# The branch projections and the output multiply of a hybrid encoder step on float16 parts instead of float32r parts, with powers of two found on the chip

## The chip, the cores and the metric

The kernel runs on one core of one Trainium2 chip. The metric is the device time of one execution in microseconds, as the median of several. A core has a matrix engine (TensorE, PE in the profile; its weight loads are the row PEld), a vector engine (VectorE, DVE), a scalar engine (ScalarE, ACT), a third elementwise engine (GpSimd, POOL) and SyncE (SP), which issues the transfers between the chip's memory and the core's on-chip buffer SBUF. PE writes its results to PSUM, a small buffer that is divided here into named banks ("a", "b", "c", "pj" and others). Each engine works its own list of instructions in order; between engines, semaphores say what may start.

## The reference

One layer of a streaming encoder, for a prompt of 2048 rows and 32 decode rows, 1024 columns wide, in float32. A projection `w_in` makes the inputs of two branches and two gates; branch A is attention over a band of chunks, branch B a gated delta rule. What concerns this change is the end:

```python
qa, ka, va, za, qkv_b, zb, a_b, b_b, gate_a, gate_b = split_projection(x @ w_in)
...
ya = (oa.reshape(bsz, t, A_WIDTH) * jax.nn.silu(za)) @ w_branch_a
...
yb = (ob * jax.nn.silu(zb)) @ w_branch_b

mix = jax.nn.sigmoid(gate_a) * ya + jax.nn.sigmoid(gate_b) * yb
y = layer_norm(ALPHA * x + mix @ w_out, ln_g, ln_b)
```

`oa * silu(za)` and `ob * silu(zb)` are called the gated values here, 512 wide each, and `mix` the merged values. `w_branch_a` and `w_branch_b` (512 x 1024) are `w_a` and `w_b` in the kernel, `w_out` is 1024 x 1024.

## The kernel before

**How the work is recorded.** Every part of the kernel is a Python generator. A small planner (class `Flow`, L155) keeps an estimated clock for each of them and for each engine, and runs the one whose clock is lowest; each instruction that it calls is recorded through one helper (L260, so that almost every row of the profile has this line) and priced by `Engine.price`. The order on each engine is therefore the order that these estimates give, fixed when the program is built. `mark` is an event, `gate(n)` a count of free buffers, `bank[...]` the gates of PSUM.

**Stages.** The rows are worked in two halves of 1024. In each half, first the jobs of branch B (phase B), then those of attention (phase A): a job is 128 columns of `w_in`, fetched (`fetch`, L585) into one of two raw slots of 512 KB, split by `divide` (L623) and multiplied by `multiply` (L664). The projections are already on float16 parts: a value is scaled by a power of two, rounded to float16 (hi), and the rest rounded again (lo); the product is hi x hi + hi x lo + lo x hi. `power` (L359) finds the power of two: ACT squares and sums each partition, a PE matmul with a constant (`tiny`) sums over the partitions, DVE adds a small number, POOL raises to the power of -1/2, and DVE masks all but the exponent.

**The merge.** When half 1's phase A is near its end, `fetch` brings `w_a` and `w_b` through the raw slots (four rows of 128 x 1024 each); `split_w` (L726) and `split` (L717) make their parts `whi` and `wlo`: ACT rounds to float32r (written `fp32r` or `f32` in rows), and POOL (even row k) or DVE (odd k) subtracts. `claim_w` (L731) waits until the buffers of both parts of h are free before it lays w_b's parts there. `last_weights` (L1962) does the same with `w_out`, in 16 pieces of 128 x 512, into `woh` and `wol`, and then loads the four layer-norm rows `l0g`, `l0b`, `lng`, `lnb`. `merge` (L2049) then works 8 blocks of 256 rows, the last of 288 with the decode rows:

- `load_g` (L2027) fetches the block's gated values of both branches, `split_g` (L2018) splits them into `ghi` and `glo`, one buffer each.
- 16 groups (f = 0 to 7, two branches) of 12 matmuls in bank "a", which has three buffers: four times whi.ghi and wlo.ghi, then four times whi.glo. DVE evacuates each with (sig + 1) x PSUM into the tile `sg` that holds the gate's values.
- `fold` (L2058): when both branches of f are there, DVE adds them (`sg<-sg`), ACT rounds the sum (`mh`), and DVE (even f) or POOL (odd f) subtracts (`ml`); `ms` holds the same for the 32 decode rows.
- the output multiply: for each 128 rows and each half of the columns (banks "pj" and "b") 24 matmuls of 512 columns, woh.mh and wol.mh for k = 0 to 7, then woh.ml. In the last block the decode rows come first, with 16 matmuls per half.
- `finish` (L2183): DVE adds PSUM times 0.5 to the row tile `xt` and does the layer norm (`lng`, `lnb`), and the row is stored.

`x_load` (L2168) prepares `xt` ahead: DVE scales the input row by its own mean and deviation (`xt<-xt,mv`), then POOL multiplies by `l0g` and adds `l0b`, two operations on 128 x 1024 one behind the other.

## Time and profile before

| | |
|---|---|
| median of 3 runs (2081.7 to 2089.64) | 2084.61 us |
| the profiled execution | 2083.65 us |
| its span, first to last instruction | 2081.6 us |
| mean granted TensorE clock | 0.988 |
| PE, DVE, ACT, POOL busy, share of the span | 95%, 72%, 47%, 30% |
| start of merge block 1 / 3 / 7 on PE | 1742.82 / 1835.30 / 2016.29 us |

Times in the profile are microseconds from the start of the span. A row of the timeline gives the start, the time, the engine, the line and the instruction with its output and inputs; in square brackets stand the idle time of the engine ahead of it and what ended that. A group's row gives the count, the busy time, the mean of one in ns, and the idle time ahead of the group's instructions. PE's matmuls are pipelined, so that their times overlap.

### The profile page before, as it was taken

What the parts mean: (1) busy time and instruction counts of PE and PEld (TensorE: products, weight loads), DVE (VectorE), ACT (ScalarE), POOL (GpSimd) and SP (SyncE); (2) the same over time, 40 slices, a digit from 0 to 9 for tenths busy, and PEclk for the clock granted to TensorE, in tenths of its full rate; (3) what the DMA queues carried; (4) which work ended last, traced back from release to release, by engine and by line L of the source; (5) the groups of instructions that cost most, each with busy time, mean ns of one, the idle gap of its engine ahead of it and who ended that gap; (6) DMA issues with size and microseconds to landing.
All of it is one profiled execution on the core that took longest, in us unless ns stands there. A gap on an engine that the chain in (4) does not pass through costs nothing. (4 is left out here: it accounts for less than half of the span.)

```text
span 2081.6 us, 41386 instructions
## 1 busy us (share of the span) xinstructions
PE 1968.6 (95%) x15098; PEld 1411.3 (68%) x15098; DVE 1499.7 (72%) x4661; ACT 978.1 (47%) x2098; POOL 633.1 (30%) x708
## 2 busy tenths in 40 slices
PE   4999999999999999998999999999999988999998
PEld 3454666766465657566667777667666777888996
DVE  7679889873377758679998986356656667666775
ACT  5565554444466667564544543355656641111110
POOL 6244333422312113243332331311011134433342
PEclk9999999999999999999999999999999999999999
DMA  3233232323423233122233233332232445433331
GB/s 119 72 92 106 75 102 57 100 80 91 116 86 111 70 92 100 65 85 72 66 89 83 77 99 84 105 92 76 72 88 88 129 137 175 132 102 122 102 116 54
DMA packets 197719, 196.49 MB, mean 94 GB/s; under 512 B 79622, under 2 KB 147570, under 8 KB 197516
## 3 DMA queue, kind: packets, MB, share of 16 engines
q1 hardware_dynamic: 197516, 193.85, 31.6%
q8 instruction: 119, 1.95, 0.4%
q14 instruction: 84, 0.69, 0.1%
HBM read 135.91 MB, written 50.53 MB: 90 GB/s over the span
## 5 line engine op out<-in xcount | busy, mean ns | idle before, releaser
L260 PE MATMUL pj<-hi,whi 128*128 128x512 f16 (+2 forms) x1992 | 644.8, 339 | 10.4 <-DVE zb L260 2.7
L260 PE MATMUL pj<-hi,wlo 128*128 128x512 f16 (+2 forms) x1952 | 635.9, 338 | 2.4 <-POOL wlo L260 2.3
L260 PEld LDWEIGHTS <-whi 128*128 128x128 f16 x3984 | 413.5, 105 | 214.5 <-issue 3.9
L260 PE MATMUL pj<-lo,whi 128*128 128x512 f16 (+2 forms) x1992 | 457.7, 340 | 0.0
L260 POOL TENSOR_TENSOR wlo<-wraw,whi 128x512 f16<-128x512 f32 x192 | 226.9, 1184 | 585.9 <-ACT whi L260 313.0
L260 PEld LDWEIGHTS <-wlo 128*128 128x128 f16 x1952 | 204.8, 105 | 111.1 <-issue 10.7
L260 ACT CAST mh<-sg 128x256 fp32r<-128x256 f32 x64 | 25.9, 406 | 279.6 <-DVE sg L260 279.6
L260 ACT CAST ph<-b 128x512 f16<-128x512 f32 (+2 forms) x224 | 93.1, 421 | 100.0 <-PE b L260 96.8
L260 DVE TENSOR_TENSOR pl<-b,ph 128x512 f16<-128x512 f32 (+2 forms) x224 | 107.7, 485 | 44.7 <-ACT ph L260 43.1
L260 PE MATMUL a<-ghi,whi 128*128 128x256 f32 (+1 forms) x512 | 132.6, 290 | 6.3 <-DVE sg L260 6.2
L260 DVE TENSOR_TENSOR sys_u<-sys_u,sys_t 128x60 f32<-128x60 f32 (+23 forms) x527 | 129.3, 251 | 6.7
L260 ACT ACTIVATE wraw<-wraw,w_scale 128x1024 f32<-128x1024 f32 (+1 forms) x98 | 111.5, 1138 | 46.6 <-DVE w_scale L260 42.9
L260 PE MATMUL a<-ghi,wlo 128*128 128x256 f32 (+1 forms) x512 | 130.3, 285 | 0.0
L260 ACT CAST whi<-wraw 128x512 f16<-128x512 f32 (+1 forms) x196 | 119.4, 612 | 20.9 <-PE pj L260 18.0
L260 DVE TENSOR_TENSOR sys_t<-sys_u,sys_p 128x60 f32<-128x60 f32 (+21 forms) x459 | 121.2, 265 | 6.1
L260 ACT ACTIVATE sb<-sb,mx,unit 128x640 f32<-128x640 f32 (+4 forms) x128 | 108.8, 851 | 20.0 <-DVE mx L260 19.7
L260 DVE SCALAR_TENSOR_TENSOR acc<-raw,cwT,acc 128x512 f32<-128x512 f32 x144 | 114.0, 792 | 5.4 <-ACT acc L260 4.4
L260 POOL TENSOR_TENSOR w_scale<-w_scale,mhalf 128x1 f32<-128x1 f32 x49 | 30.9, 631 | 269.3 <-DVE w_scale L260 204.2
L260 PE MATMUL b<-ident,sb 128*128 128x128 f32 x560 | 100.6, 279 | 5.3 <-ACT sb L260 2.2
L260 PEld LDWEIGHTS a<-ghi,whi 128*128 128x128 f32 x512 | 98.0, 191 | 9.0 <-DVE sg L260 7.8
L260 ACT COPY v_t<-o 128x64 f32<-128x64 f32 x132 | 27.7, 210 | 161.1 <-PE o L260 133.3
L260 PEld LDWEIGHTS a<-ghi,wlo 128*128 128x128 f32 x512 | 97.8, 191 | 0.3
(350 smaller groups left out, 4221.8 us busy)
## 6 DMA issues: line engine op xcount, KB each, us to landing
wraw<-in_w_in SPq DMA_DIRECT2D x192, 256.0 KB
sg<-sig SPq DMA_DIRECT2D x112, 128.0 KB
sig<-sig SPq DMA_DIRECT2D x44, 256.0 KB
sys_p<-sol_p SPq DMA_DIRECT2D x17, 512.0 KB
x<-in_x_p SPq DMA_DIRECT2D x16, 512.0 KB
xt<-in_x_p SPq DMA_DIRECT2D x16, 512.0 KB
out_y_p<-xt SPq DMA_DIRECT2D x16, 512.0 KB
glo<-g SPq DMA_DIRECT2D x14, 512.0 KB
```

Source lines behind the costliest of these rows:

```text
L260: r = f(*a, **k)
```

## The change

All float32r parts become float16 parts, which need a power of two ahead of the rounding:

- **w_a and w_b**: each row k has its own power, `b_scale` (a Square with a sum into `b_sq`, `power`), its reciprocal `b_inv`, and the least of the four, `b_min` (`weigh`). w_a's four rows and eight extra fetches of w_out (`measure_o`, which only squares and sums them for the one power `o_scale`) are fetched between the jobs of half 1's phase A, one ahead of each of twelve jobs, through the same raw slots. w_b is fetched behind the jobs as before, but waits for only one of the two buffers of h.
- **w_out**: split with `o_scale`, all 16 `wo` tiles in one pool.
- **gated values**: `load_g` has two buffers for the parts and a raw tile per branch. ACT squares both branches (into the parts' low buffers, which are overwritten later), `power` takes both sums at once, and the least of power x `b_min` gives the block's unit; each row k of the gated values is scaled by unit x `b_inv`, so that all products of a group have one scale.
- **merged values**: scaled by the constant `MSMALL` (2^-18). `finish` multiplies by a value per block that undoes all this, instead of 0.5.
- **the split** itself: for odd k, ACT writes the scaled hi and DVE makes lo in one operation (x times scale minus hi); for even k, ACT scales in place, ACT rounds, and POOL subtracts. The low parts `ml` and `ms` are now all made by DVE.

```diff
-    def power(out, sums):
+    def power(out, sums, n=1):
...
+        more = [measure_o] * KD + [split_a] * NP
         for job in jobs:
+            if job.half and job.key and job.key[0] == 0 and job.key[1] > 0:
+                f = more.pop(0)
+                if f is split_a and len(more) == NP - 1:
+                    yield from claim_w(0)
...
+                yield raw_gate
+                raw = wpool.tile([P, KD, P], F32, tag="wraw", bufs=NRAW, name="raw_more")
+                raw = raw[:].rearrange("p k n -> p (k n)")
+                flow.start(f(k, raw, dma(raw, (w_a if f is split_a else w_out)[k * P:(k + 1) * P, :])))
+                yield
...
-        for br, w in enumerate((w_a, w_b)):
-            yield from claim_w(br)
...
+        yield from claim_w(1)
+        for k in range(NP):
...
+            flow.start(split_w(1, k, wr, dma(wr, w_b[k * P:(k + 1) * P, :])))
...
+    def measure_o(k, raw, t):
+        yield t
+        S.activation(out=raw, in_=raw, func=AF.Square, accum_out=o_sq[:, k:k + 1])
+        raw_gate.give()
+        o_left[0] -= 1
+        if not o_left[0]:
+            yield
+            V.tensor_reduce(out=o_sq[:, KD:], in_=o_sq[:, 0:KD], axis=AX.X, op=ALU.add)
+            yield
+            yield from power(o_scale[:, 0:1], o_sq[:, KD:])
...
+    def split(hi, lo, x, sc, eng, m):
+
+        if eng is V:
+            S.activation(out=hi, in_=x, func=AF.Copy, scale=sc)
+            m[0].done()
+            yield
+            V.scalar_tensor_tensor(out=lo, in0=x, scalar=sc, in1=hi, op0=ALU.mult, op1=ALU.subtract)
+        else:
+            S.activation(out=x, in_=x, func=AF.Copy, scale=sc)
+            yield
+            S.copy(out=hi, in_=x)
+            m[0].done()
+            yield
+            G.tensor_tensor(out=lo, in0=x, in1=hi, op=ALU.subtract)
+        m[1].done()
...
+        S.activation(out=lo[:, k], in_=wr, func=AF.Square, accum_out=sq)
+        yield
+        yield from power(sc, sq)
+        flow.start(weigh(br, k))
+        for c in range(2):
+            cs = slice(c * 512, (c + 1) * 512)
+            yield from split(hi[:, k, cs], lo[:, k, cs], wr[:, cs], sc, V if k % 2 else G,
+                             (mark(), w_ready[br, k, c]))
+            yield
+        raw_gate.give()
...
     def claim_w(br):
         if br:
-            for g in h_free:
-                yield g
+            yield h_free[0]
...
-    g_slot, m_slot, x_slots = gate(1), gate(1), gate(3)
+    g_slot, m_slot, x_slots = gate(2), gate(1), gate(3)
...
+                S.activation(out=glo[:, :, 0:n], in_=raw[:, :, 0:n], func=AF.Square, accum_out=gs[:, br:br + 1])
+                yield
+
+            yield from power(gs[:, 2:4], gs[:, 0:2], 2)
+            for k in b_known:
+                yield k
+            V.tensor_tensor(out=gs[:, 2:4], in0=gs[:, 2:4], in1=b_min[:], op=ALU.mult)
+            yield
+            V.tensor_reduce(out=gs[:, 4:5], in_=gs[:, 2:4], axis=AX.X, op=ALU.min)
...
-                eng = G if f % 2 else V
-                S.copy(out=mh[:, f], in_=parts[0][:, 0:FB])
+                S.activation(out=mh[:, f], in_=parts[0][:, 0:FB], func=AF.Copy, scale=MSMALL)
                 m_ready[0][f].done()
                 yield
-                eng.tensor_tensor(out=ml[:, f], in0=parts[0][:, 0:FB], in1=mh[:, f].bitcast(F32), op=ALU.subtract)
+                V.scalar_tensor_tensor(out=ml[:, f], in0=parts[0][:, 0:FB], scalar=MSMALL, in1=mh[:, f], op0=ALU.mult,
+                                       op1=ALU.subtract)
...
-            V.scalar_tensor_tensor(out=xt[:rows, cs], in0=part, scalar=0.5, in1=xt[:rows, cs],
+            V.scalar_tensor_tensor(out=xt[:rows, cs], in0=part, scalar=unit[:rows], in1=xt[:rows, cs],
```

The planner sets the order of everything anew from the first extra fetch on (about 1325 us). Three places matter below.

DVE in a merge block in the middle, around the scaling of the first of its two row tiles, before (`sg<-sg,a` evacuates a group, `sg<-sg` adds the branches):

```order
L260 TENSOR_SCALAR xt<-xt,mv 128x1024
L260 SCALAR_TENSOR_TENSOR sg<-sg,a 128x256
L260 TENSOR_TENSOR sg<-sg 128x256
L260 SCALAR_TENSOR_TENSOR sg<-sg,a 128x256
L260 TENSOR_TENSOR sg<-sg 128x256
L260 TENSOR_TENSOR ml<-sg,mh 128x256
L260 SCALAR_TENSOR_TENSOR sg<-sg,a 128x256 x2
```

and the same place after the change:

```order
L262 TENSOR_SCALAR xt<-xt,mv 128x1024
L262 SCALAR_TENSOR_TENSOR sg<-sg,a 128x256
L262 SCALAR_TENSOR_TENSOR ml<-sg,mh 128x256
L262 TENSOR_TENSOR sg<-sg 128x256
L262 SCALAR_TENSOR_TENSOR ml<-sg,mh 128x256
L262 SCALAR_TENSOR_TENSOR sg<-sg,a 128x256 x3
L262 TENSOR_TENSOR sg<-sg 128x256
```

Between two evacuations there stand now two subtractions and an add, where before there were an add or an add and a subtraction.

POOL in the same block, before (`m` is the layer norm's small value):

```order
L260 TENSOR_TENSOR xt<-xt,l0g 128x1024
L260 TENSOR_TENSOR ml<-sg,mh 128x256
L260 TENSOR_TENSOR xt<-xt,l0b 128x1024
L260 TENSOR_TENSOR ml<-sg,mh 128x256 x2
L260 TENSOR_TENSOR xt<-xt,l0g 128x1024
L260 TENSOR_TENSOR xt<-xt,l0b 128x1024
L260 TENSOR_TENSOR ml<-sg,mh 128x256
L260 TENSOR_TENSOR glo<-glo,ghi 128x256 x4
```

and after:

```order
L262 TENSOR_TENSOR m_23256<-m_23256,mhalf 128x1
L262 TENSOR_TENSOR xt<-xt,l0g 128x1024
L262 TENSOR_TENSOR xt<-xt,l0b 128x1024
L262 TENSOR_TENSOR xt<-xt,l0g 128x1024
L262 TENSOR_TENSOR xt<-xt,l0b 128x1024
L262 TENSOR_TENSOR gs<-gs,mhalf 128x2
L262 TENSOR_TENSOR m_23617<-m_23617,mhalf 128x1
L262 TENSOR_TENSOR glo<-graw,ghi 128x256 x4
```

The four `ml` of the block have left POOL, and the operations with `l0g` and `l0b` stand next to each other; a small operation of the gated values' power (`gs`) has come in.

PE at the first matmuls of the branch projections (`a<-ghi,whi`), before (`pj<-lo,whi` are the last projections, `b<-ident,sb` transposes of attention):

```order
L260 MATMUL pj<-lo_9880,whi 128x272
L260 MATMUL b<-ident,sb 128x128 x4
L260 LDWEIGHTS whi
L260 MATMUL pj<-lo_9880,whi 128x272
L260 LDWEIGHTS whi
L260 MATMUL pj<-lo_9880,whi 128x272
L260 MATMUL a<-ghi,whi_20624 128x256
L260 MATMUL a<-ghi,wlo_20625 128x256
L260 MATMUL b<-ident,sb 128x128
```

and after (`c<-vt,ph` and `c<-vt,pl` are attention's products of probabilities and values):

```order
L262 LDWEIGHTS ph
L262 MATMUL c<-vt_20108,ph 128x64
L262 LDWEIGHTS pl
L262 MATMUL c<-vt_20108,pl 128x64
L262 MATMUL b<-ident,sb 128x128 x8
L262 LDWEIGHTS whi_18612
L262 MATMUL a<-ghi,whi_18612 128x256
L262 LDWEIGHTS wlo_18613
L262 MATMUL a<-ghi,wlo_18613 128x256
```

The first of them stood right behind the last projection and stands now some 210 rows behind it, with that much of attention moved ahead; a matmul with float16 weights has a row of its own for the load. And between the last of block 0's branch matmuls and its first output matmul, where nothing stood before, PE has now the power of the gated values of block 2:

```order
L262 LDWEIGHTS whi_21332
L262 MATMUL a<-glo,whi_21332 128x256
L262 MATMUL b<-gs,tiny 128x2
L262 LDWEIGHTS mh
L262 MATMUL pj<-woh_22280,mh 128x512
```

This one small matmul (`b<-gs`) waits for ACT's two Squares of that block.

130 lines of the change are left out of this document (78 added, 52 removed).

## The prediction

> **What bounds the kernel now.** I read the page's totals first, then the table of windows, then PE's waits, then PE's timeline.
>
> ```profile
> span 2081.6 us, 41386 instructions
> PE 1968.6 (95%) x15098; PEld 1411.3 (68%) x15098; DVE 1499.7 (72%) x4661; ACT 978.1 (47%) x2098; POOL 633.1 (30%) x708
> ...
> core 0: us, PE busy (x) PEld busy (x) DVE busy (x) ACT busy (x) POOL busy (x), PEclk, DMA share, GB/s
> 1340.00:1660.00 320.00, 312.16 (x2866) 221.88 (x2863) 201.44 (x694) 188.71 (x446) 46.56 (x40) 1.00 0.31 90
> 1660.00:1680.00 20.00, 18.32 (x171) 13.45 (x168) 14.77 (x53) 14.29 (x34) 5.01 (x4) 0.92 0.27 86
> 1680.00:1700.00 20.00, 17.78 (x163) 15.85 (x162) 11.44 (x39) 5.85 (x16) 1.80 (x2) 0.83 0.21 59
> 1700.00:1740.00 40.00, 32.89 (x168) 26.77 (x169) 28.52 (x40) 15.20 (x30) 16.49 (x16) 0.96 0.77 252
> 1820.00:1860.00 40.00, 40.00 (x270) 36.97 (x269) 28.88 (x47) 2.85 (x7) 14.08 (x10) 1.00 0.33 106
> ...
> PE pj L260 <- ACT mh L260: 1.5, 3, 0.8
> PE a L260 <- DVE sg L260: 1.3, 2, 1.2
> PE pj L260 <- POOL ms L260: 0.6, 1, 0.6
> ```
>
> PE is busy 95% of the span, and its order is fixed, so the time is PE's work plus the holes in it. The windows give three stages that the change touches. From 1340 to 1660 (half 1, phase A) PE is busy 312 of 320. From 1660 to 1740 (the end of attention and merge block 0) it has its holes: 18.32 + 17.78 + 32.89 = 69.0 of 80. From then on the merge blocks run full: 40.00 of 40 in the window of block 3, and the last three rows, PE's waits from 1760 to 2082, come to 3.4 us in all. The profiled execution took 2083.65 us, of which 2081.6 is the span; the median is 2084.61, 0.05% more, so a sum made on the profile holds for the median.
>
> **What float16 saves on PE.** The columns are the start, the time and the instruction.
>
> ```profile
> 52.00 0.27 PE L260 MATMUL pj<-hi,wlo 128*128 128x256 f16 x1
> ...
> 53.20 0.27 PE L260 MATMUL pj<-hi,whi 128*128 128x256 f16 x1
> ...
> 1001.19 0.38 PE L260 MATMUL pj<-hi,whi 128*128 128x512 f16 x1
> ...
> 1002.92 0.38 PE L260 MATMUL pj<-hi,whi 128*128 128x512 f16 x1
> ...
> 1836.72 0.28 PE L260 MATMUL a<-ghi,whi 128*128 128x256 f32 x1
> ...
> 1846.68 0.28 PE L260 MATMUL a<-ghi,whi 128*128 128x256 f32 x1
> ...
> 1864.16 0.39 PE L260 MATMUL b<-woh,mh 128*128 128x512 f32 x1
> ...
> 1867.56 0.40 PE L260 MATMUL b<-wol,mh 128*128 128x512 f32 x1
> ```
>
> The durations of pipelined matmuls overlap, so I go by the distance of their starts. Float32r at 256 columns: 84 matmuls (seven groups of 12) from 1836.72 to 1846.68, 0.1186 us each. Float16 at 256: 11 steps from 52.00 to 53.20, 0.1091. Float32r at 512: 15 steps from 1864.16 to 1867.56, 0.2267. Float16 at 512: 8 steps from 1001.19 to 1002.92, 0.2163. The merge has 8 blocks x 16 groups x 12 = 1536 matmuls of the first kind and 8 x 96 + 32 (the decode rows) = 800 of the second. So PE's work shrinks by 1536 x 0.0095 + 800 x 0.0104 = 14.6 + 8.3 = **22.9 us at most**, 1.8 + 1.0 = 2.8 a block. The rest of the change adds work and waits; the question is how much of 22.9 is left.
>
> **Phase A: +4.** Twelve fetches of 512 KB (eight of w_out for measure_o, four of w_a) go between the jobs of half 1, and each adds work: the weights' eight rows and w_out's total need nine powers, of which w_a's four and w_out's fall in this stage, w_b's four in the next.
>
> ```profile
> L260 PE MATMUL b<-w_sq,tiny 128*128 128x1 f32 x98 | 17.1, 244 | 6.9 <-ACT whi L260 5.7 <-DVE kd_bd L260 1.2
> L260 ACT ACTIVATE whi<-wraw 128x1024 f16<-128x1024 f32 x49 | 51.7, 1054 | 67.9 <-PE pj L260 37.2 <-issue 21.4 <-DMA wraw<-in_w_in 4.6
> L260 ACT ACTIVATION_READ_ACCUMULATOR whi<-wraw 128x1 f32 x49 | 9.2, 187 | 0.0
> ```
>
> A power's matmul (two records each, 49 powers) costs PE (17.1 + 6.9) / 49 = 0.49 us with its wait; five of them (w_a's and w_out's) are 2.4 here. A Square is 1.054 + 0.187 = 1.24 us of ACT, 12 of them 14.9, beside 320 - 188.71 = 131 us in which ACT has nothing to do; DMA is at a share of 0.31. That hides them, but the fetches take turns in the two raw slots with the w_in jobs, and POOL and DVE get the subtractions of w_a. I add 1.5 for such collisions and take +4; the range is 0 (the powers slip into holes) to +10 (each of 12 fetches holds a job up by 0.5 beyond that).
>
> **The end of attention and block 0's branch projections: 0.**
>
> ```profile
> 1660.97 0.37 PE L260 MATMUL a<-ghi,whi 128*128 128x256 f32 x1
> ...
> 1693.54 0.32 PE L260 MATMUL b<-ident,ob 128*128 128x128 f32 x1 [0.66 <-DVE ob L260]
> ...
> 1713.59 0.39 PE L260 MATMUL pj<-woh,mh 128*128 128x512 f32 x1
> ...
> L260 ACT CAST woh<-wr 128x512 fp32r<-128x512 f32 x6 | 3.5, 615 | 0.0
> ...
> L260 PE MATMUL a<-ghi,whi 128*128 128x256 f32 x24 | 7.5, 333 | 0.0
> ...
> PE a L260 <- DVE sg L260: 4.8, 4, 2.1
> PE b L260 <- ACT woh L260: 1.8, 2, 1.3
> ```
>
> Before, the first a-matmul stands right behind the last projection (1660.97) and fills holes of attention; the last row of attention is at 1693.54, and block 0's 16 groups end at 1713.59. The group row is of 1660.9 to 1693.5: 24 matmuls of this kind, 4 to a group, so six groups lie beside attention and ten behind. After the change the first scale of the gated values needs the powers of all four w_b rows, so in PE's order the first a-matmul stands behind most of attention's transposes and p.v products (the PE rows of the section on the change): I put it at about 1683, by the last pair of w_b plus Square, power, the small DVE steps and the casts. What is queued behind it on PE is the rest of attention. From 1683, the 16 groups' 16 x 1.31 = 21 us end at 1704, which leaves 9.6 us up to 1713.59 for the rest of attention between them. In all, PE has 1.8 less to do here by its steps and 2.0 more by w_b's four powers. So 0. Below, before waited 4.8 for sg here and the groups now stand together, so -4 is possible; above, the weights' Squares add 5 us to an ACT that is at 14.29 of 20 from 1660 to 1680, so +8.
>
> **Block 0's output multiply: +2.** The gain is 96 x 0.0104 = 1.0. Against it: in PE's order the power for block 2 (b<-gs) now stands right ahead of the first output matmul. Its two Squares write the buffers that block 0's last groups read, so about two of 1.24 us fall behind those groups: 2.5 with the hop. w_out's even rows get a second ACT pass, 8 x 0.615 us (the woh row) = 4.9, where PE already waited 1.8 for woh; I count 0.5 of it. Sum +2; -1 if the Squares are early, +6 if the casts come through whole.
>
> **Blocks 1 to 7: -3.5 instead of -20.**
>
> ```profile
> 1842.41 0.81 DVE L260 TENSOR_SCALAR xt<-xt,mv 128x1024 f32<-128x1024 f32 x1
> ...
> 1843.30 2.39 POOL L260 TENSOR_TENSOR xt<-xt,l0g 128x1024 f32<-128x1024 f32 x1 [5.02 <-DVE xt L260]
> ...
> 1843.46 2.50 DVE L260 TENSOR_TENSOR sg<-sg 128x256 f32<-128x256 f32 x1
> ...
> 1846.33 0.42 DVE L260 TENSOR_TENSOR sg<-sg 128x256 f32<-128x256 f32 x1
> ...
> 1846.54 0.82 POOL L260 TENSOR_TENSOR ml<-sg,mh 128x256 fp32r<-128x256 f32 x1 [0.85 <-POOL xt L260]
> ...
> 1857.72 2.46 POOL L260 TENSOR_TENSOR xt<-xt,l0b 128x1024 f32<-128x1024 f32 x1
> ...
> 1858.40 2.07 DVE L260 TENSOR_TENSOR ml<-sg,mh 128x256 fp32r<-128x256 f32 x1
> ...
> 1742.82 0.28 PE L260 MATMUL a<-ghi,whi 128*128 128x256 f32 x1
> ...
> 1789.57 0.28 PE L260 MATMUL a<-ghi,whi 128*128 128x256 f32 x1
> ...
> 1835.30 0.28 PE L260 MATMUL a<-ghi,whi 128*128 128x256 f32 x1
> ...
> 1880.52 0.28 PE L260 MATMUL a<-ghi,whi 128*128 128x256 f32 x1
> ```
>
> The add of the branches (sg<-sg) takes 0.42 us at 1846.33 and 2.50 at 1843.46, when POOL's l0g runs; ml takes 2.07 beside l0b. So DVE's operations with two SBUF inputs stand still until POOL's long one ends, and everything behind them in DVE's order too, the evacuation of PSUM included. The Trainium skill ("SBUF — State Buffer", section "🔬 SBUF: two separate sides") says that VectorE and GpSimd share one pair of ports, held for a whole instruction. The trace agrees (2.50 against 0.42); the rule speaks against moving ml to DVE, and without it the blocks would bring the full 2.8 each.
>
> Block 3 takes 1880.52 - 1835.30 = 45.2 us; 192 x 0.1186 + 96 x 0.2267 = 44.5. After, in us from its start and by the order after: DVE's scaling of x comes at 7.6 and l0g runs from 8.4 to 10.8. The ml of f=1, new on DVE, waits for it until 11.0. POOL has no ml between any more, so l0b runs from 10.8 to 13.3 and stops DVE's next add until 13.5; ACT's cast and the next ml follow until 14.5, and only then group 6's evacuation, until 14.9. PE has three banks: it ends group 8 at 9 x 1.31 = 11.8 and **waits for group 6's bank until 14.9, 3.1 us**. The second pair of l0g and l0b falls on the last groups and ends ahead of what PE needs. The groups end at 192 x 0.1091 + 3.1 = 24.1; mh of f=7 is there at 26.9 and needed at 24.1 + 14 x 0.2163 = 27.1; the output multiply takes 96 x 0.2163 = 20.8 and the power 0.3: 45.2, as before. Saved and lost are equal: 0 for blocks 2 to 6. Block 1 started at 1742.82 and has 46.7 us before (to 1789.57); I let it come to 45.2, -1.5. Block 7 loads no next x tiles for a full block and gets 2.0 of its 2.8. Sum -3.5. The unseen duration is ml as an operation with a scalar: at least the 0.42 of today's, at most the 0.81 of the scaling of x at four times the columns; I take 0.42, since the shape is the same. The wait of 3.1 could be 0.9 (a single stop of 2.1 instead of two) or 4.6 (both pairs of a block stop PE), so each of the five blocks lies in -2 to +1.5.
>
> **Sum.** 2083.65 + 4 + 0 + 2 - 3.5 = 2086.15: **2086 us**, no change that can be measured. A measurement of this kernel can tell about 0.5% from none: 2074.2 and 2095.0 are the bounds.
>
> **Rivals.**
> *PE stays the bound in the merge.* POOL's pair could start later or earlier against PE, so that three banks cover it; today they cover 2.5 us stops (40.00 of 40 busy). Then 22.9 arrive and phase A's 4 stay: 2083.65 - 22.9 + 4 = 2065. Against it stands the order: two POOL operations back to back. The Trainium skill ("Perfetto Trace Analysis", section "Identifying the Most-Contended Engine") judges TensorE by the share of weight loads; it is 36.97 of 40 here, and by that rule shorter loads would come through in full. The row bears it out for before, not for DVE's new order. 0.24.
> *Slower: the weights arrive late.* One chain decides: w_b's last fetch, Square, power, minimum, scale, casts, then the first a-matmul. If that matmul starts at 1700 and not 1683, behind attention's end, the 16 groups end at 1700 + 20.9 = 1720.9, 7.3 late; the 24 ACT passes of w_out then stand behind the gated values' and the 4.9 us come through, with 1.5 more where w_b's powers find no cover: 2086 + 14 = 2100. It decides from a start of 1693.5 on, where nothing of attention is left to cover it. For it: ACT at 14.29 of 20. Against it: w_a's casts leave this stretch. 0.22.
> *Float16 steps no faster here* (weight loads and matmuls in separate instructions, at the step of 0.1186 and 0.2267): the blocks' 1.8 + 1.0 are lost, while the wait shrinks to 14.9 - 9 x 1.42 = 2.1; 8 x 1.8 more, 2101. The float16 rows speak against it. 0.06.
>
> **Chances and range.** Forecast 0.48 (2074 to 2096), first rival 0.24 (2058 to 2073), second 0.22 (2096 to 2108), third 0.06. The range of 2062 to 2104 leaves out about a quarter of the first rival, a third of the second and half of the third: under 0.2. Faster: 0.24 + 0.02 = 0.26; slower: 0.22 + 0.06 - 0.01 = 0.27; same: 0.47.
>
> **What would show it.** Starts 0.109 and 0.216 apart in the merge; blocks of about 45 us with 3 us of PE waiting for DVE's sg in each, and no wait for mh; POOL's l0g and l0b adjacent, a DVE ml of some 2 us beside each; first a-matmul near 1683 (1661 on the time of before) plus phase A's 4; a wait of PE ahead of b<-gs before block 0's first output matmul. Blocks of 42.5 us would make it wrong on the fast side, a first a-matmul 30 us behind the last projection on the slow side.

## The result, and the profile after

The changed kernel takes **2104.14 us** (median of 4 runs, 2103.61 to 2109.47) against 2084.64 of the kernel before: the ratio is 1.0095, with a 95% interval of 1.0075 to 1.0114. It is slower by 0.95%, just above the upper end of the forecast range (2104) and beyond its bound for "no change". The profiled execution took 2103.61 us.

The totals and the same windows as before, of the changed kernel:

```profile
span 2101.8 us, 41640 instructions
PE 1961.4 (93%) x15132; PEld 1315.7 (63%) x15132; DVE 1526.1 (73%) x4784; ACT 1039.8 (49%) x2210; POOL 610.2 (29%) x689
...
1340.00:1660.00 320.00, 306.90 (x2743) 216.09 (x2742) 194.36 (x676) 199.41 (x455) 45.45 (x42) 0.99 0.35 103
1660.00:1680.00 20.00, 18.02 (x187) 13.87 (x185) 16.32 (x66) 16.50 (x37) 3.53 (x4) 1.00 0.26 85
1680.00:1700.00 20.00, 17.32 (x150) 12.03 (x151) 11.95 (x56) 14.42 (x37) 3.40 (x4) 0.66 0.03 8
1700.00:1740.00 40.00, 26.70 (x252) 22.00 (x250) 28.38 (x67) 28.28 (x62) 15.22 (x16) 0.93 0.63 198
1820.00:1860.00 40.00, 37.10 (x230) 23.18 (x229) 26.87 (x53) 9.14 (x23) 11.06 (x10) 0.96 0.35 112
```

PE has 306.9 us of work where it had 312.2 in phase A, 26.7 of 40 where it had 32.9 around block 0's output, and 37.1 where it had 40.0 from 1820 to 1860, in the merge blocks. Each stage has got holes. The granted clock (third column from the end) is 0.66 from 1680 to 1700, where it was 0.83; the last section comes back to that. PE's timeline at the marks between the stages, of the kernel before (only its first row is new) and of the changed kernel; the first row is a projection of phase B, ahead of every changed instruction:

```profile
1199.64 1.09 PE L260 MATMUL pj<-lo,whi 128*128 128x272 f16 x8
```

```profile
1202.75 1.09 PE L262 MATMUL pj<-lo,whi 128*128 128x272 f16 x8
...
1675.98 0.28 PE L262 MATMUL pj<-lo,whi 128*128 128x272 f16 x1
...
1701.52 0.27 PE L262 MATMUL a<-ghi,whi 128*128 128x256 f16 x1 [1.19 <-ACT ghi L262]
...
1711.62 0.27 PE L262 MATMUL b<-ident,ob 128*128 128x128 f32 x1
...
1740.84 0.58 PE L262 MATMUL b<-gs,tiny 128*128 128x2 f32 x2 [7.40 <-ACT glo L262]
1741.29 0.59 PE L262 MATMUL pj<-woh,mh 128*128 128x512 f16 x1
```

The end of that first projection (1200.7 before, 1203.8 changed) is called **the mark** from here on. In the profiles of this study it lies between 1199.2 and 1208.0, with the same instructions ahead of it (in e1, e5 and e11 the first 50 us stand in a slightly different order), so stages are compared from the mark and not from the start. From the mark, the last projection ends 12.0 us later than before (472.4 against 460.5), attention 15.0 later (507.8 against 492.8), and block 0's branch matmuls 16.6 later (529.6 against 513.0). Block 0's output, up to the start of block 1, takes 31.5 instead of 29.1, and blocks 1 to 7 take 328.6 instead of 330.5. The sum is +17.1 by the mark; the medians differ by 19.5. The wait of 7.40 us in that list is for ACT, whose timeline shows the Squares of block 2's gated values behind passes for w_out and mh:

```profile
1737.77 0.42 ACT L262 ACTIVATE mh<-sg 128x256 f16<-128x256 f32 x1 [0.92 <-DVE sg L262]
1738.10 0.60 ACT L262 CAST woh<-wr 128x512 f16<-128x512 f32 x1
1738.60 1.05 ACT L262 ACTIVATE glo<-graw 128x1024 f16<-128x1024 f32 x1
```

So nearly all of the loss lies **ahead of block 0's output multiply**, and the seven blocks that the change was to shorten by 20 us bring 1.9.

Where that went is seen in PE's waits from 1780 to the end (total, times, longest), and in POOL's and DVE's timelines in block 4:

```profile
PE a L262 <- DVE sg L262: 17.3, 8, 2.9
PE pj L262 <- ACT mh L262: 0.4, 1, 0.4
```

```profile
1909.34 0.81 DVE L262 TENSOR_SCALAR xt<-xt,mv 128x1024 f32<-128x1024 f32 x1
1910.07 0.42 DVE L262 SCALAR_TENSOR_TENSOR sg<-sg,a 128x256 f32<-128x256 f32 x1
...
1910.23 2.35 POOL L262 TENSOR_TENSOR xt<-xt,l0g 128x1024 f32<-128x1024 f32 x1 [5.51 <-DVE xt L262]
...
1910.40 2.47 DVE L262 SCALAR_TENSOR_TENSOR ml<-sg,mh 128x256 f16<-128x256 f32 x1
...
1912.66 2.40 POOL L262 TENSOR_TENSOR xt<-xt,l0b 128x1024 f32<-128x1024 f32 x1
...
1912.79 2.56 DVE L262 TENSOR_TENSOR sg<-sg 128x256 f32<-128x256 f32 x1
...
1916.18 1.08 DVE L262 SCALAR_TENSOR_TENSOR sg<-sg,a 128x256 f32<-128x256 f32 x3
...
1916.64 0.27 PE L262 MATMUL a<-ghi,whi 128*128 128x256 f16 x1 [2.90 <-DVE sg L262]
```

The two DVE operations that take 0.42 us alone stand for 2.47 and 2.56 beside POOL's two, three evacuations wait behind them, and PE waits 2.90 us for the first.

### The profile page after: what moved, and what is told of

Same layout as the page of the kernel before. It is cut to its first block, busy times and chain, and to the rows that moved or that the text cites. A ratio compares the mean times of both kernels' runs of the same rounds, so it can differ in the third digit from the quotient of the medians.

```text
span 2101.8 us, 41640 instructions
## 1 busy us (share of the span) xinstructions
PE 1961.4 (93%) x15132; PEld 1315.7 (63%) x15132; DVE 1526.1 (73%) x4784; ACT 1039.8 (49%) x2210; POOL 610.2 (29%) x689
## 5 line engine op out<-in xcount | busy, mean ns | idle before, releaser
L262 PEld LDWEIGHTS <-whi 128*128 128x128 f16 x5008 | 516.6, 104 | 234.4 <-issue 5.9
L262 PE MATMUL pj<-hi,whi 128*128 128x512 f16 (+2 forms) x1992 | 647.3, 340 | 10.5 <-DVE zb L262 2.7
L262 PEld LDWEIGHTS <-wlo 128*128 128x128 f16 x2464 | 256.6, 104 | 147.9 <-issue 35.8
L262 PE MATMUL a<-ghi,whi 128*128 128x256 f16 (+1 forms) x512 | 124.7, 280 | 24.0 <-DVE sg L262 22.6
L262 ACT ACTIVATE mh<-sg 128x256 f16<-128x256 f32 x64 | 26.6, 417 | 224.3 <-DVE sg L262 224.3
L262 ACT CAST whi<-wraw 128x512 f16<-128x512 f32 (+1 forms) x196 | 119.4, 612 | 23.8 <-PE pj L262 21.0
L262 PE MATMUL a<-ghi,wlo 128*128 128x256 f16 (+1 forms) x512 | 124.7, 281 | 0.0
L262 POOL TENSOR_TENSOR w_scale<-w_scale,mhalf 128x1 f32<-128x1 f32 x49 | 30.9, 631 | 269.2 <-DVE w_scale L262 206.4
L262 ACT COPY v_t<-o 128x64 f32<-128x64 f32 x132 | 27.8, 211 | 160.6 <-PE o L262 133.9
L262 DVE CUSTOM_DVE_ANT_0 sb<-a,bias 128x320 f32<-128x320 f32 (+4 forms) x128 | 61.5, 486 | 48.0 <-PE a L262 47.5
L262 PEld LDWEIGHTS b<-ident,sb 128*128 128x128 f32 x560 | 70.1, 144 | 33.3 <-PE a L262 3.9
```

What stands on the lines that cost most here:

```text
L262: r = f(*a, **k)
```

## The experiments

All times are medians in us, beside runs of the kernel before on the same chip (medians 2086.0 to 2087.6). The stages are read off PE's timeline: from the mark to the end of the last projection, to attention's last transpose, and to the end of block 0's branch matmuls; then from there to block 1's start (output 0), and blocks 1 to 7. "changed+" means the changed kernel with one edit.

| kernel | time | ratio to before, 95% | last proj. | att. | branch 0 | output 0 | blocks 1-7 |
|---|---|---|---|---|---|---|---|
| before | 2086 | | 460.5 | 492.8 | 513.0 | 29.1 | 330.5 |
| changed | 2104.14 | 1.0095 [1.0075, 1.0114] | 472.4 | 507.8 | 529.6 | 31.5 | 328.6 |
| e3 changed+ x_load on DVE | 2081.82 | 0.9979 [0.9959, 0.9999] | 471.1 | 506.4 | 528.5 | 30.7 | 305.3 |
| e4 changed+ odd ml on POOL | 2097.36 | 1.0068 [1.0048, 1.0088] | 472.1 | 507.4 | 532.0 | 30.7 | 318.4 |
| e9 before, x_load on DVE | 2078.87 | 0.9959 [0.9944, 0.9974] | 460.4 | 489.6 | 508.4 | 27.8 | 323.4 |
| e2 changed+ load of g later | 2114.10 | 1.0128 [1.0090, 1.0166] | 472.1 | 507.5 | 529.3 | 22.5 | 348.3 |
| e1 changed+ w_out not measured | 2096.99 | 1.0052 [1.0035, 1.0069] | 463.7 | 500.5 | 525.7 | 30.1 | 328.8 |
| e5 changed+ fetched, not squared | 2094.01 | one run | 472.6 | 504.3 | 524.5 | 30.9 | 329.2 |
| e7 changed+ measured earlier | 2102.78 | 1.0075 [1.0045, 1.0104] | 469.3 | 504.8 | 530.2 | 29.3 | 328.3 |
| e10 changed+ own slot | 2104.73 | 1.0091 [1.0058, 1.0123] | 465.5 | 506.7 | 528.3 | 31.5 | 328.4 |
| e11 changed+ branch powers constant | 2094.08 | 1.0031 [1.0017, 1.0046] | 477.8 | 505.3 | 524.1 | 31.5 | 327.4 |
| e13 all weights' powers constant | 2092.62 | 1.0028 [1.0013, 1.0042] | 456.9 | 497.5 | 517.0 | 31.8 | 328.8 |
| e14 e13, w_a behind the jobs | 2087.82 | 1.0008 [0.9992, 1.0023] | 455.0 | 494.8 | 513.6 | 30.7 | 328.2 |
| e15 e13, g's power constant too | 2065.88 | 0.9896 [0.9864, 0.9927] | 458.9 | 487.9 | 506.5 | 28.9 | 313.2 |
| e18 e15 with g's Squares | 2080.69 | 0.9979 [0.9962, 0.9996] | 459.8 | 491.6 | 510.4 | 30.3 | 325.9 |
| e19 e15 with g's power | 2083.50 | 0.9996 [0.9979, 1.0012] | 459.1 | 489.5 | 508.5 | 29.0 | 329.9 |
| e8 three edits | 2081.53 | 0.9968 [0.9954, 0.9982] | 469.3 | 504.8 | 530.3 | 23.8 | 311.7 |
| e12 all measured early | 2077.68 | 0.9969 [0.9950, 0.9987] | 463.1 | 504.8 | 524.4 | 24.7 | 315.0 |
| e16 e12, first x on POOL | 2083.44 | 0.9987 [0.9973, 1.0000] | 464.3 | 506.6 | 525.9 | 24.5 | 318.2 |
| e17 e16, power as changed | 2080.00 | 0.9959 [0.9945, 0.9973] | 463.8 | 505.8 | 525.9 | 31.1 | 307.2 |

Each stage is read off a single profile. Up to "branch 0" the changed kernel, e2 and e3 have the same program, and read 528.5 to 529.6 (e4, which differs there in block 0's ml only, 532.0); before and e9 have the same program up to there too, and read 513.0 and 508.4. So differences under some 5 us there mean nothing by themselves.

### The holes in the blocks: e3, e4, e9

```diff
-        V.tensor_scalar(out=xt[:rows], in0=xt[:rows], scalar1=mv[:rows, gt, 0:1],
-                        scalar2=mv[:rows, gt, 1:2], op0=ALU.subtract, op1=ALU.mult)
+        V.scalar_tensor_tensor(out=xt[:rows], in0=xt[:rows], scalar=mv[:rows, gt, 0:1], in1=rowv["l0g"][:rows],
+                               op0=ALU.subtract, op1=ALU.mult)
         yield
-        eng = V if gt < 2 else G
-        eng.tensor_tensor(out=xt[:rows], in0=xt[:rows], in1=rowv["l0g"][:rows], op=ALU.mult)
-        yield
-        eng.tensor_tensor(out=xt[:rows], in0=xt[:rows], in1=rowv["l0b"][:rows], op=ALU.add)
+        V.scalar_tensor_tensor(out=xt[:rows], in0=xt[:rows], scalar=mv[:rows, gt, 1:2], in1=rowv["l0b"][:rows],
+                               op0=ALU.mult, op1=ALU.add)
```

> The changed kernel, but x_load runs as two operations on DVE ((x - mean) times l0g, then times the deviation plus l0b), none on POOL. Theory A (POOL's l0g and l0b stop DVE's two-input operations, and that makes the 2.9 us holes before a-groups in blocks 2 to 5): the waits of PE for sg fall from 17.3 us (1780 to the end) to under 5, DVE's ml and sg<-sg are all near 0.42, blocks 3 to 5 take 42 to 43 us instead of 45 to 46.7, time 2086 to 2090. Theory B (DVE is simply full: 3.5 us a block more of it): the waits for sg stay at 12 or more, time 2100 to 2108.

e3's waits from 1780 to the end, and its group of ml in blocks 1 to 6; below them the same group of the changed kernel:

```profile
PE a L262 <- DVE sg L262: 1.8, 5, 0.4
...
L262 DVE SCALAR_TENSOR_TENSOR ml<-sg,mh 128x256 f16<-128x256 f32 x53 | 22.3, 420 | 10.0 <-ACT mh L262 10.0
```

```profile
L262 DVE SCALAR_TENSOR_TENSOR ml<-sg,mh 128x256 f16<-128x256 f32 x54 | 45.2, 838 | 8.1 <-ACT mh L262 7.3
```

DVE has more work and ml takes half the time, 420 ns instead of 838; the waits for sg fall from 17.3 to 1.8, blocks 1 to 6 take 42.1 to 42.3 us each, and the kernel gains 22. Theory A holds, and the gain is some 4 us larger than its range: with the holes, three stretches at half clock went too, which the last section shows.

e4 puts ml for odd f back on POOL:

```diff
+                if f % 2:
+                    S.activation(out=parts[0][:, 0:n], in_=parts[0][:, 0:n], func=AF.Copy, scale=MSMALL)
+                    yield
+                    S.copy(out=mh[:, f], in_=parts[0][:, 0:FB])
...
+                    G.tensor_tensor(out=ml[:, f], in0=parts[0][:, 0:FB], in1=mh[:, f], op=ALU.subtract)
...
```

> The changed kernel, but for odd f ACT scales the merged sum in place, rounds it, and POOL subtracts, as before the change; PE's order is nearly the same as in the changed kernel. Theory A (the move of ml to DVE and the two POOL operations side by side make the holes): the waits for sg fall from 17.3 to under 8, time 2092 to 2096. Theory B (it is not where ml stands, POOL's own operations stop DVE as long): the waits for sg stay between 13 and 20, time 2101 to 2107.

The time is 1.4 above theory A's range; the waits for sg fall to 5.4, but 7.4 for mh come in, since ACT now needs two passes ahead of it. So moving ml made a part of the holes; the rest went only with POOL's operations, in e3.

e9 is the same x_load edit in the kernel before the change.

> The kernel before the change (float32r), with x_load on DVE alone. It tells how much of what x_load on DVE gave the changed kernel (22 us) has to do with float16. Theory A (float32r's blocks are bound by PE: 44.5 of 45.2 us are matmuls): blocks 44.5 to 45, time 2079 to 2084 against 2086. Theory B (POOL's stops cost both kernels alike): blocks near 43, time near 2066.

Theory A for the blocks: blocks 2 to 6 take 44.6 us each, where they took 44.9 to 45.8. The gain, 8.7 against runs on the same chip (2087.6), is a little above its range. In blocks 1 to 7 taking these operations from POOL gives float32r 7.1 us (330.5 to 323.4) and float16 23.3 (328.6 to 305.3).

### The wait ahead of block 0's output: e2

```diff
-            g_slot.give()
...
                     flow.start(finish(w, gt, rows, c, ps, unit[:, 6:7], b == NB - 1 and t == 1))
+                if t == 0:
+                    g_slot.give()
```

> The changed kernel, but a block gives its place for the next gated values' load after its first 128 output rows and not ahead of them, so that the power for block 2 no longer stands ahead of block 0's first output matmul. Theory A (the 7.40 us wait ahead of b<-gs is the power's alone): the hole before block 0's first output matmul shrinks to under 2, block 1 starts 6 us earlier against block 0's last branch matmul, time near 2098. Theory B (w_out's pieces are late anyway, ACT casts them until 1738 and two more at 1749): waits for woh and wol take its place, block 1 starts less than 3 us earlier, time 2101 to 2104.

The wait went and output 0 fell from 31.5 to 22.5, more than either theory gave; w_out's pieces were in time. But the kernel became 10 us slower: the splits of the gated values now fell into the next block's groups, and the waits for sg from 1780 to the end rose from 17.3 to 30.3 us. e16 (below) records only block 2's power later, and e17 is e16 without that: output 0 is 24.5 in e16 and 31.1 in e17, blocks 1 to 7 are 318.2 and 307.2. The wait is worth nothing by itself; its place is taken in block 1, which takes 54.4 us in e16 and 43.7 in e17.

### Ahead of block 0: what is measured, and how

e1 leaves the measuring of w_out out; e5 keeps its eight fetches and leaves out only the Squares and their power.

```diff
-        more = [measure_o] * KD + [split_a] * NP
+        more = [None] * KD + [split_a] * NP
...
+    V.memset(o_scale[:, 0:1], 1024.0)
+    V.memset(o_scale[:, 1:2], 0.5 / MSMALL / 1024.0)
+    o_known.done()
```

> The changed kernel without the eight fetches and Squares of w_out in phase A: o_scale is the constant 1024 (the power that the weights of this case have), all else as changed. In the changed kernel the last projection is at 1676.3, 15.1 later than before; 3.1 of that is there already at 1203, ahead of any changed instruction. Theory A (the extra fetches and their ACT work delay the attention chain in phase A, 12 us for 12 fetches): two thirds come back, last projection near 1668, time near 2096. Theory B (the 12 us are chance of the order that the planner finds and of halved clock windows): last projection within 3 us of 1676, time within 3 of 2104.

> The changed kernel with the eight fetches of w_out in phase A, but without their Squares and the power (o_scale is the constant 1024): the slot is given back when the fetch lands. Measured by the stretch from the projection that ends near 1315 to the last one: 349.3 us before, 361.3 changed, 352.5 without fetches and Squares. Theory A (the Squares stand in ACT's order ahead of attention's softmax): with the fetches alone the stretch is 352 to 355. Theory B (the fetches hold the raw slots and delay the jobs' weights): 358 to 362.

e1 gains 7.2, as theory A said, and its last projection comes 8.7 sooner. In e5 it doesn't come sooner at all (472.6; in the measure of the expectation, 361.4): the fetches hold it, not the Squares, theory B of e5. Yet e5's attention and block 0 end as early as e1's within the spread, and its one time is no worse. What the Squares and their power cost is seen there, 3.5 us at attention's end and 5.1 at block 0's, and in the one time, 10 us; the first two are no more than the spread of a profile.

e10 gives these fetches a slot and a stream of their own; e7 keeps the slots and takes one fetch ahead of each job behind phase B.

```diff
+    def measure_o():
+        for i in range(2 * KD):
+            k, c = divmod(i, 2)
+            yield more_gate
+            raw = wpool.tile([P, 512], F32, tag="more", bufs=1, name="raw_more")
+            yield dma(raw[:], w_out[k * P:(k + 1) * P, c * 512:(c + 1) * 512])
+            S.activation(out=raw[:], in_=raw[:], func=AF.Square, accum_out=o_sq[:, i:i + 1])
+            more_gate.give()
+            yield
```

> The changed kernel, but w_out is measured by a stream of its own through a slot of its own (half rows of 128x512, 16 fetches), so that no fetch of it takes one of the two raw slots from the jobs; Squares, power and bytes stay. Measured from the projection that ends near 1204 to the last projection: 460.5 us before, 472.5 changed, 463.7 without measuring, 472.6 with the fetches alone. Theory A (the raw slots: a fetch pushes the next job's weights back, and attention loses the projection matmuls that fill its holes): 463 to 466. Theory B (the bytes of the fetches, or the Squares): 470 to 474.

```diff
-            if job.half and job.key and job.key[0] == 0 and job.key[1] > 0:
-                f = more.pop(0)
...
+            if len(more) > NP:
+                if tail:
+                    f = more.pop(0)
+            elif job.half and job.key and job.key[0] == 0 and job.key[1] == NP - 1:
+                f = more.pop(0)
+            if job.half and job.key == (1, NP - 1, 3):
+                tail = True
```

> The changed kernel with w_out measured earlier, one fetch ahead of each of the eight jobs behind phase B (about 1240 to 1345, where ACT is busy for 24 of 60 us and attention has hardly begun), w_a's four fetches where they were. Theory A (it is attention's chain of ACT and DVE that the Squares delay): the stretch from the projection near 1315 to the last is 353 to 356 instead of 361.3 and nothing is lost ahead of it, time near 2097. Theory B (each of the fetches costs about a microsecond wherever it is): the last projection stays at 1675 to 1679, time near 2104.

e10's last projection comes 6.9 sooner, theory A for the slots; but attention ends where it did (506.7) and the time is the changed kernel's. So the last projection was the wrong thing to watch: what the jobs win, attention's rest loses. e7's stretch is 355.9 in the measure of the expectation, theory A, but 2.2 us are lost ahead of it and attention ends only 3.0 sooner: 1.4 us of gain, theory B in the time.

The remaining edits replace powers by constants. In e11 those of the branch weights, in e13 all weights' (so that w_out's extra fetches go, too), in e14 w_a goes behind the jobs again, and in e15 the gated values' Squares and power go too; e18 and e19 bring back one of the two.

```diff
+    for br, v in enumerate((256.0, 2048.0)):
+        V.memset(b_scale[:, br], v)
...
-        S.activation(out=lo[:, k], in_=wr, func=AF.Square, accum_out=sq)
-        yield
-        yield from power(sc, sq)
-        flow.start(weigh(br, k))
```

> The changed kernel, but the powers of w_a's and w_b's rows are constants (256 and 2048, near those that it finds): their Squares and powers are left out, so that the first scale of the gated values waits for no w_b row. Measured by the time from the last projection to the first a-matmul (25.3 us in the changed kernel: 1676.3 to 1701.5) and from the projection near 1204 to the end of block 0's branch matmuls (513.1 before, 529.6 changed). Theory A (the chain of w_b's power, minimum, scale and casts, at whose every step an in-order engine has other work, holds the first a-matmul back): first a-matmul 10 to 15 us sooner, the second number 518 to 522, time near 2094. Theory B (attention's own chain sets the end, the a-matmuls only fill it): the second number stays above 526.

> The changed kernel with all weights' powers constant: no extra fetch of w_out, no Squares and powers of w_a, w_b and w_out; w_a is still fetched between the jobs, the gated values' power is still found. Theory A (measuring the weights is the whole loss ahead of block 0): from the projection near 1204 to the end of block 0's branch matmuls 511 to 516, as before the change (513.1). Theory B (the gated values' Squares, their second ACT pass and the order do a part of it): 518 to 524.

e14, on top of e13:

```diff
-        more = [None] * KD + [split_a] * NP
+        more = [None] * (KD + NP)
...
-        yield from claim_w(1)
...
+        for br, w in enumerate((w_a, w_b)):
+            yield from claim_w(br)
...
```

> All weights' powers constant as in e13, and w_a's four rows fetched behind the jobs as before the change, not between them. From the projection near 1204 to the end of block 0's branch matmuls: 517.0 in e13, 508 to 513 before. Theory A (w_a's fetch and its split beside attention cost the rest): 509 to 514. Theory B (they cost nothing there): 515 to 520, or more if w_a's late arrival now holds the first a-matmul.

e15, on top of e13; e18 keeps the first of these lines, e19 the `power` (from constant sums):

```diff
-                S.activation(out=glo[:, :, 0:n], in_=raw[:, :, 0:n], func=AF.Square, accum_out=gs[:, br:br + 1])
...
-            yield from power(gs[:, 2:4], gs[:, 0:2], 2)
...
-            V.tensor_reduce(out=gs[:, 4:5], in_=gs[:, 2:4], axis=AX.X, op=ALU.min)
+            V.memset(gs[:, 4:5], 32768.0)
```

> All weights' powers constant as in e13, and the gated values' unit constant too (their Squares and their power are left out; scaling and both parts stay). Theory A (the gated values' Squares and power cost the rest): the same stretch 509 to 514 instead of 517.0; theory B: 515 to 519. In both the 7.5 us wait ahead of block 0's first output matmul goes, since there is no power; if w_out's pieces do not take its place, from the end of block 0's branch matmuls to block 1 it takes 24 to 26 instead of 31.8.

> As e15 (all powers constant), but the gated values' Squares are done and not used; no power. Theory A (the Squares on ACT and their place in its order): most of the 26.7 us comes back, time 2085 to 2093. Theory B (the chain of small operations through PE, DVE and POOL): time 2064 to 2072. In the stretch from the projection near 1204 to the end of block 0's branch matmuls, 506.5 in e15 and 517.0 in e13: A 514 to 518, B 505 to 510.

> As e15, but the gated values' power is found, from constant sums in place of the Squares' (the result is the same unit). Theory A (the Squares): 2064 to 2072. Theory B (the power's chain): 2085 to 2093. If both parts only move the planned order so that DVE's operations meet POOL's lock in the blocks: the blocks' waits for sg are near 18 us in one of the two kernels and near 5 in the other, whatever the time ahead of block 0.

In e11 the first a-matmul follows the last projection at once, and branch 0 ends 5.5 sooner than in the changed kernel, the time 10 lower: theory A in the time, 2 short in the stage. e13 gains 11.5; its 517.0 lies between the two theories. e14 gives 513.6 and 4.8 us, theory A. e15 gains **26.7 us** on e13: branch 0 ends at 506.5, earlier than theory A had it, the wait of 7.45 us ahead of output 0 is gone (output 0 still takes 28.9, since waits for mh, woh and wol come in), and blocks 1 to 7 take 313.2. With e18 and e19 either half alone brings more than half of that back (2080.7 and 2083.5), which fits neither theory. Most of what they bring back lies in blocks 1 to 7 (12.7 and 16.7 us); up to the end of branch 0 it is 3.9 and 2.0, within the spread. PE's waits from 1780 to the end, of e15, e18 and e19 in turn:

```profile
PE a L262 <- DVE sg L262: 4.7, 3, 2.5
```

```profile
PE a L262 <- DVE sg L262: 17.4, 8, 2.9
```

```profile
PE a L262 <- DVE sg L262: 18.4, 8, 3.0
```

The waits for sg are back in both, against the third theory, which had them in one of the two. What differs in the blocks is one exchange in DVE's order. e15, block 4:

```profile
1880.66 0.81 DVE L262 TENSOR_SCALAR xt<-xt,mv 128x1024 f32<-128x1024 f32 x1
1881.38 0.42 DVE L262 SCALAR_TENSOR_TENSOR ml<-sg,mh 128x256 f16<-128x256 f32 x1
...
1881.54 2.47 POOL L262 TENSOR_TENSOR xt<-xt,l0g 128x1024 f32<-128x1024 f32 x1 [7.02 <-DVE xt L262]
...
1884.16 2.56 DVE L262 TENSOR_TENSOR sg<-sg 128x256 f32<-128x256 f32 x1
```

Here ml stands right behind the scaling of x and is on its way 0.16 us ahead of POOL; in the changed kernel an evacuation stands between them, ml comes 0.17 behind POOL and waits. So it is in blocks 1 to 6 of e15, while in blocks 2 to 5 of e13, e18 and e19 this ml starts behind POOL and takes 2.0 to 2.5 us. With one stop less, PE's three banks bridge the rest. The planner's prices know nothing of these stops, so an added instruction elsewhere can tip this order; the exchange alone was not tried.

### Versions: e8, e12, e16, e17

e8 is e3 and e7 with this, which records the power's matmul for block 2 behind block 0's first output tile:

```diff
+            if b == 2:
+                yield first_out
             yield from power(gs[:, 2:4], gs[:, 0:2], 2)
...
+                    if b == t == c == 0:
+                        first_out.done()
```

> Three edits together: x_load on DVE, w_out measured behind phase B, and the matmul of block 2's power recorded only when block 0's first output matmuls are. If they are independent: 2081.8 (x_load on DVE) less 8 (measuring) less 5 (the wait of 7 ahead of b<-gs, of which w_out's pieces take 2) is 2069. If w_out's late pieces take the whole place of the b<-gs wait: 2074. If measuring early gains nothing: 2077 to 2082.

The edits are not independent: 2081.53, the last case of the expectation, no better than x_load on DVE alone. Output 0 is 7 us shorter than in e3 and blocks 1 to 7 are 6.4 longer.

In e12 the stream of e10 goes over all three weights, and the branch rows' powers come out of it at once:

```diff
+    def know_b():
+        sq, sc = (x[:].rearrange("p b k -> p (b k)") for x in (b_sq, b_scale))
+        V.tensor_reduce(out=sq, in_=b_part[:], axis=AX.X, op=ALU.add)
+        yield
+        yield from power(sc, sq, 2 * NP)
...
```

> w_a, w_b and w_out are all measured by the stream with a slot of its own during phase A (one power for the eight branch rows), w_a and w_b are fetched behind the jobs as before the change and split at once; x_load on DVE, and block 2's power behind block 0's first output matmuls. If slot and chain are the two causes of the loss ahead of block 0: from the projection near 1204 to the end of block 0's branch matmuls 508 to 516 (508.5 in the float32r kernel with x_load on DVE), blocks 42.3, time 2062 to 2070, below the 2078.9 of the float32r kernel with x_load on DVE. If only one of them is: 2070 to 2079.

It takes 2077.68 us; e9, the float32r kernel with x_load on DVE, 2078.87, and their intervals overlap. By the marks, e12 wins 8.4 us on e9 in blocks 1 to 7 and 3.1 in output 0, and loses 16.0 ahead of them: attention's end (504.8) has hardly moved, so the slot and the chain of w_b were not the two whole causes.

e16 gives the first two row tiles back to POOL, e17 takes the later power out of it again:

```diff
+        if gt < 2:
+            V.tensor_scalar(out=xt[:rows], in0=xt[:rows], scalar1=mv[:rows, gt, 0:1],
+                            scalar2=mv[:rows, gt, 1:2], op0=ALU.subtract, op1=ALU.mult)
+            yield
+            G.tensor_tensor(out=xt[:rows], in0=xt[:rows], in1=rowv["l0g"][:rows], op=ALU.mult)
+            yield
+            G.tensor_tensor(out=xt[:rows], in0=xt[:rows], in1=rowv["l0b"][:rows], op=ALU.add)
...
```

> e12 (everything measured early, x_load on DVE, block 2's power later), but for the first two row tiles DVE only scales and POOL multiplies and adds. In e12 PE waits 5.14 us at 1753.81 while DVE works off four such operations and the first rows' layer norm, and block 1 takes 50.8 instead of 42.3. Theory A (DVE's clump of x tiles): block 1 takes 45 to 47, time near 2073. Theory B (POOL's operations stop DVE as long): block 1 stays at 49 to 52, time 2076 to 2080.

> e16 without the edit that records block 2's power later, so that it stands ahead of block 0's first output matmul as in the changed kernel. Theory A (moving the power only shifts the wait into block 1): block 0's output multiply begins some 7 us later, and block 1 takes 42 to 43; start of block 2 within 2 us of e16's. Theory B: block 2 starts 4 us or more later than in e16.

e16 is slower than e12: block 1 takes 54.4, longer than even theory B had it. From the mark, block 2 begins at 604.8 in e16 and at 600.6 in e17: recording the power later costs 4 us here, neither theory. e9 and e12 both beat the kernel before, by 0.4 and 0.3%; e15, in which no power has to be found, gains 1.0%, but with a lucky order in the blocks, and its constants fit these weights and inputs only.

## Why the prediction was wrong

- **PE's steps**: right. In the changed kernel 7 steps from 1910.96 to 1911.73 are 0.110 each, and 12 output matmuls from 1925.81 to 1928.40 are 0.216.
- **Blocks 1 to 7, -3.5**: right in the mechanism; that the size fits (-1.9) is in part luck. The hole of 3.1 us that was to stand ahead of group 9 is there, 2.9, in each of blocks 2 to 5, and the waits for mh are down to 0.4; e3 shows the cause. The rule of the Trainium skill ("SBUF — State Buffer", section "🔬 SBUF: two separate sides") on the ports that DVE and POOL share decided it, as the prediction used it: ml is 2.47 beside POOL's operation, 0.42 in e3. But blocks 2 to 6, put at 0, lost 4.4 us in all: blocks 2, 3 and 6 took 46.7 to 47.5 and not 45, for a reason in the last section. Block 1 (43.4, not 45.2) and block 7 (3.0 us gained, not 2.0) made up for a part of it.
- **Block 0's output, +2**: right in size (+2.4) by luck, since two errors cancel. The wait ahead of b<-gs is 7.40 and not 2.5, since ACT's two Squares stood behind passes for w_out and mh until 1738.60; of the old waits there (4.3 us, for woh, mh and wol) only 1.0 is left.
- **The end of attention, 0**: +4.6 from the last projection on, inside its range. The first a-matmul came 25.3 us behind the last projection; 22 were forecast.
- **Phase A, +4**: here it failed. It was +12.0 to the last projection, outside its range of 0 to 10, and with the step above +16.6 up to block 0's output, where +4 was forecast. Two terms were wrong. The first is the collisions in the raw slots, put at 1.5: w_out's fetches alone hold the last projection back by 8.9 (472.6 in e5, which has no Squares of w_out, against 463.7 in e1, which has no such fetches either). That didn't reach the time, though: with a slot of their own (e10) the projection comes 6.9 sooner, and the kernel is no faster. The step that failed in the time is the cover: 14.9 us of Squares "beside 320 - 188.71 = 131 us in which ACT has nothing to do", which "hides them".
- **What finding the powers cost up to block 0's output**: with the weights' powers constant (e13) this stretch is 517.0, and with the gated values' as well (e15) 506.5, no more than before: finding the powers, w_out's fetches included, is the whole loss there, 529.6 - 506.5 = 23 us, and no one part of it. It is 3.9 without w_out's (e1), 5.5 without the branch weights' (e11), 12.6 without both (e13), and 10.5 more without the gated values' (e15 against e13); the single parts are near the spread of a profile, the sums are not. The prediction's sum has no term at all for the gated values' Squares and powers of the first two blocks, which stand in this stretch (PE's `b<-gs` at 1631.20 and 1712.82). w_a's early fetch adds 3.4 (e14 against e13), within the spread, though the time falls by 4.8. How the cover failed is not shown: ACT's idle time in phase A lies between the steps of attention's chain, which runs through PE, ACT and DVE in turn, but which of the added instructions delays which of attention's was not tried, and the planner lays out the order anew with each edit. A part of the 23 us can also be PE at half clock behind the new holes (last section).
- **The rivals**: "the weights arrive late" had the side and the number (2100, from a first a-matmul at 1700; it came at 1701.52). Its mechanism holds for a part: without w_b's chain (e11) the kernel gains 10 us, while 12 us of the delay were there already at the last projection. "PE stays the bound" had the number of e15, 2065.88 where 2065 was forecast, but by another sum: e15 finds no power, wins 6.5 us ahead of block 0's output where the rival had lost 4, and has a lucky order on DVE. "Float16 steps no faster" falls with the steps above.

## What to carry to other kernels

ACT was idle 40% of phase A, and the work put there was not free. Where a stage is a chain through several in-order engines, price added work by leaving it out in a copy, and watch the end of the chain: in e10 the last projection came 6.9 us sooner and the kernel not at all. A faster matmul pays only as far as the evacuation behind it keeps up; where another engine can lock that one out, the first thing to move is the locking operation (22 us in e3, 8.7 in e9), before the matmuls are touched. And a scale that has to be found on the chip costs more than its instructions: the steps were worth 22.9 us, and with all powers constant (e15) the kernel was 38 us faster, 15 of them in the blocks, where the order had one stop less.

## What the runs showed of the hardware

Holes in PE cost more than their length. Windows of the changed kernel, cut to 3.4 us behind three of the holes, with the granted clock in the third column from the end; and ten microseconds around the hole of block 4; below them the first window in e3, which has no hole there:

```profile
1823.30:1826.70 3.40, 3.40 (x17) 2.43 (x17) 1.67 (x6) 0.42 (x1) 0.00 (x0) 0.51 0.74 217
1871.10:1874.50 3.40, 3.40 (x18) 2.46 (x17) 1.44 (x5) 0.65 (x2) 0.00 (x0) 0.50 0.82 243
1914.00:1924.00 10.00, 7.36 (x68) 6.60 (x68) 7.76 (x18) 1.67 (x4) 2.61 (x2) 1.00 0.54 161
2007.60:2011.00 3.40, 3.40 (x19) 2.42 (x17) 1.59 (x6) 0.83 (x2) 0.00 (x0) 0.51 0.52 162
```

```profile
1823.30:1826.70 3.40, 3.40 (x34) 3.05 (x32) 2.92 (x7) 0.42 (x1) 0.00 (x0) 1.00 0.52 149
```

Behind the holes of 2.9 us that end at 1823.22 and 1869.94, and the one of 2.27 that ends at 2006.41, PE ran at half clock for one stretch of 3.4 us, and got half as many matmuls done (17 and 18, against 34 in e3); behind the equal holes that end at 1916.64 and 1961.69 it didn't. Each such stretch costs 1.7 us, which is what blocks 2 and 3 (46.7) took more than blocks 4 and 5 (45.1 and 45.0). The Trainium skill ("TensorE: Matmul & The Clock Gate", section "🔬 Part 1: The HAM clock gate (the "warmup" mystery)") has a free-running window of about 3.4 us by which the clock is halved after an idle window. The length and the half agree; that it takes a whole idle window doesn't, since 2.27 us were enough here. Whether a hole is hit seems to depend on where in the window it falls, which may also be why the mark moves by 9 us between profiles (27.3 to 47.8 us ahead of it are at half clock); that was not tried apart.

The same happened at the end of attention. Of the changed kernel, and of the kernel before:

```profile
1680.00:1693.60 13.60, 12.96 (x90) 8.62 (x91) 5.66 (x26) 8.44 (x20) 3.40 (x4) 0.50 0.02 6
```

```profile
1676.60:1683.40 6.80, 6.80 (x40) 3.90 (x37) 3.49 (x11) 2.69 (x7) 2.49 (x2) 0.50 0.01 2
```

From the mark to the end of branch 0, PE stood at half clock for 23.9 us in the changed kernel, 10.2 in the kernel before, 13.7 in e13 and 3.4 in e15. If PE was the bound in all of that, half of each difference is the clock's: at most 6.8 of the 16.6 us lost there, and 10.2 of the 23 that e15 wins back. This is an upper estimate from these stretches. Since half clock came behind holes, it is a part of how the added work cost time and not a cause beside it; how large a part was not tried.
